# Layer 1's experts: outputs added as two float32r parts, the sum and the next gather placed between matrices, weight loads of one run per partition

## The chip, the cores and the metric

The kernel runs on one core of one Trainium2 chip. Its time is the device time of one execution in microseconds (us); the median of the runs shown counts. Engines: PE (TensorE; PEld is its weight load), DVE (VectorE), ACT (ScalarE), POOL (GpSimd), SP (SyncE, which issues the loads). "fp32" is float32; float32r is a second type that matmuls here are given; the kernel writes a float32 value as a sum hi + lo of two float32r values where it uses it.

## The reference

One sequence of 512 latent tokens and 256 context tokens of width 1024 goes through two layers (an mLSTM mixer and a retention mixer, each followed by experts) and then through a second block of another kind. What the change touches is the experts of layer 1, which act on the latent tokens alone:

```python
def expert_choice_ffn(h, router, w_gate, w_up, w_down):   # abridged: each of 16 experts picks its 64 best tokens
    aff = softmax(h @ router)                 # [512 tokens, 16 experts]
    gates, idx = top_k(aff.T, 64)             # an expert's 64 tokens and their gates
    xe = h[idx]                               # gather
    ye = (silu(xe @ w_gate) * (xe @ w_up)) @ w_down      # three matrices 1024 x 1024 of an expert
    return zeros.at[idx].add(gates[..., None] * ye)      # add to the tokens' rows
x = x + mod_l[5] * expert_choice_ffn(h_lat, ...)
```

Layer 0 does the same for 64 latent and 32 context tokens of an expert, and its mixer takes a shift and a scale, columns of `silu(c) @ ada_w[0]`.

## The kernel before

Layer 1's experts are `moe1`. X, the residual, lies in SBUF as four tiles of 128 tokens by 1024. Experts run one after the other; the first and the last stand alone for the gather, those between go in groups of two (1 and 2, 3 and 4, ...).

*Gather* (L1257). For a group a 0/1 matrix oh (L1249, DVE) picks the tokens, and per block of 128 features 4 matmuls bring the picked tokens, features on the partitions, into PSUM "tp" (three buffers), from where ACT (L1261) or DVE (L1259) writes them with gain and shift to xT (one buffer). 32 matmuls gather one group. *Facts* (L1279): small matmuls 64x17 that bring the gates and the numbers of the picked tokens, copied to mo_gi (L1281).

*Matrices* (`expert_gemm`, L866). A 1024x1024 matrix comes in four slots of 1 MiB, each one load on SP's queue (L833); a slot serves four matmuls of 64 tokens by 512 columns, and when they are done it is free for the next load. There are 18 slots. PSUM "pl" takes gate and up, "dl" down. Between up and down stands `expert_hidden`: silu on ACT (L1154), times up on DVE (L1155), four transposes (L1159) and a copy to hTl (L1160).

*Combine*. After down, y = dl * gate * mod5 goes to Y by two 64-partition DVE instructions (L1292); POOL copies the token numbers to ic (L1294). After each odd expert, so for a pair (0 and 1, 2 and 3, ...), a 0/1 matrix sh is made from ic (L1298, two DVE instructions), and for each of 8 pieces of X (4 token tiles by 2 halves of 512 columns) one float32 matmul sh x Y into PSUM "cb" (two buffers, L1302) and one DVE addition to X (L1304) follow:

```python
cb = ps.tile([128, 512], F32, name="cb", bufs=2)
nc.tensor.matmul(cb, sh[:, b, 128 * t:128 * t + 128], Y[b], start=True, stop=True)
nc.vector.tensor_add(xs, xs, cb)
```

What sets the order of the instructions is not the code alone: a scheduler of the tile framework orders each engine's instructions by what they depend on and by its own estimate of when things are ready, so that gathers come between the matmuls of a matrix in pieces. The order of each engine is fixed when the program is built. In the trace a float32 matmul 128x512 or 64x512 is two PE records (8 records are one slot of 4 matmuls), one of 128x128 also two, a float32r matmul one.

`ada_part` computes layer 0's shift and scale at the start, with two 512 KB loads per slot, of runs of 1 KB (L241).

Of the kernel before, what the change touches and what calls it, by code (L numbers as in the profile page):

```python
# [6 lines left out]
F32 = mybir.dt.float32  # L7
# [16 lines left out]
class Pool:  # L24
    """A tile pool that is closed by hand."""
# [11 lines left out]
class Ring:  # L37
    """Tiles of several pools in turn, as many of each as it has."""
# [9 lines left out]
class Net:  # L48
    NW = 4   # slots of the weight stream
    NB0, NB1 = (3, 3), (4, 2)   # slots beside them while the experts run, early and late, by layer  # L50
# [44 lines left out]
    def rstd(self, pool, ss, n, dim):  # L95
        """1 / sqrt(ss / dim + eps) for ss [128, n]."""
# [19 lines left out]
    def ada_open(self):  # L116
        """Pools of the modulation's products, which run beside other phases."""
# [20 lines left out]
    def fill(self, n=1):  # L138
        """Emits n steps, n may be a fraction, of the work that was put aside."""
# [10 lines left out]
    def ada_chunk(self, i, j, nr, p, tile):  # L150
        """Columns [1024 j, 1024 j + 1024) of silu(c) @ ada_w[i] + ada_b[i] for the first nr of both c:
        the products and their sum over row blocks on VectorE, a step a pair of them, the sum over partitions by
        tile(), of PSUM. The gates (j = 2 and 5) go to DRAM, else features are on the partitions."""
# [29 lines left out]
        else:  # L183
# [7 lines left out]
            # tp[:, 256 r + 128 b + 32 q + any]: block 2 q + b of the features, row r  # L191
# [12 lines left out]
    def ada_mix(self):  # L204
        """Of layer 1's mixer, the shift and scale; a step a row block."""
# [18 lines left out]
        # tp[:, 128 b + 64 c + 32 q + r]: chunk c, block 4 q + b of its columns, row r  # L224
# [34 lines left out]
    def load_weights(self, src):  # L259
        """src ([128, a, b] view of DRAM) in a slot."""  # L260
# [19 lines left out]
    def split_evac(self, pool, ps, hi, lo, A=None, B=None):  # L280
        """hi + lo = ps * A + B, from PSUM."""
# [11 lines left out]
    def mm3(nc, out, lh, rh, start, stop):  # L293
        """(lh0 + lh1)^T (rh0 + rh1) without the product of the low parts."""
# [61 lines left out]
    def normalise(self, pool, out, x, g=None):  # L356
        """out = x / rms(x) (* g), for a token tile [128, 1024]."""
# [129 lines left out]
    def mlstm_gates(self, G, gp):  # L487
        """Of both directions, what the chunks need of the gates, into self.gates: constants, and by direction the order of the
        chunks, the row terms (Fl - m, and exp(Fl - m + m before the chunk)) in three bfloat16 parts, and the
        columns ig - Fl, exp(suffix + ig - m at the end), exp(-m) and the state's decay."""  # L490
# [18 lines left out]
        def parts(x, name):  # L509
            """Three bfloat16 parts of x [8, 768] that add up to it, at partitions 0, 32 and 64."""  # L510
# [182 lines left out]
    def mlstm_finish(self, t, y, sigo, ng, pool):  # L693
        """Norm of each head of token tile t, times gain and sigmoid(o), in place."""
# [36 lines left out]
    def route_tile(self, x, r, dst, pp, ps, warm=None):  # L731
        """Softmax affinities of the token tile x [128, 1024] of kind r into dst [128, 16]; returns 1 / rms."""
# [8 lines left out]
        nc.scalar.activation(ss, self.epsc, AF.Sqrt)   # the function loaded ahead; ss is overwritten  # L741
# [23 lines left out]
    def rank_open(self, pp, kinds):  # L765
        """What the ranks of the first expert's tokens need: by kind of token, of which there are kinds[r] tiles."""
# [49 lines left out]
    def expert_stream(self, i, order):  # L816
        """The weights of layer i's experts, two row blocks of 128 a slot, by order: pairs of expert and matrix. open(slot, n,
        behind) starts loading into n further slots, once behind [1, 1] is there, not to hold up the load that brings it;
        get() is the next; done() frees the oldest one in use for a load."""
# [5 lines left out]
        def load(slot, behind=None):  # L825
# [7 lines left out]
            nc.sync.dma_start(t, I["moe_w_" + w][i, e, 128 * k:128 * k + 256, :].rearrange("(k p) n -> p k n", p=128))  # L833
# [1367 lines left out]
```

## Time and profile before

| | |
|---|---|
| runs, median (lowest to highest) | 2660.91 us, 3 runs (2656.61 to 2661.49) |
| profiled execution, first to last instruction | 2661.6 us |
| PE busy of it | 2543.3 us (96%) |
| DVE, ACT, POOL busy | 1069.2, 671.2, 564.7 us |
| mean granted clock of TensorE | 0.981 |
| bytes moved | 585.00 MB, 220 GB/s |

Layer 0's experts lie at 600 to 1100 us, layer 1's at 1517 to 2043 us, and the second block follows. A row of the windows gives for a stretch its length, each engine's busy time with its instructions in brackets, the granted clock as a share of full speed, the mean busy share of the 16 DMA engines and the bytes per time. A row of the waits gives the engine and line that waited, what released it, the total, the number of times and the longest. Idle time that the rows name is to the modelled end of the record before, so a gap read from start to start is longer.

### The profile page before, as it was taken

What the parts mean: (1) busy time and instruction counts of PE and PEld (TensorE: products, weight loads), DVE (VectorE), ACT (ScalarE), POOL (GpSimd) and SP (SyncE); (2) the same over time, 40 slices, a digit from 0 to 9 for tenths busy, and PEclk for the clock granted to TensorE, in tenths of its full rate; (3) what the DMA queues carried; (4) which work ended last, traced back from release to release, by engine and by line L of the source; (5) the groups of instructions that cost most, each with busy time, mean ns of one, the idle gap of its engine ahead of it and who ended that gap; (6) DMA issues with size and microseconds to landing.
All of it is one profiled execution on the core that took longest, in us unless ns stands there. A gap on an engine that the chain in (4) does not pass through costs nothing.

```text
span 2661.6 us, 36603 instructions
## 1 busy us (share of the span) xinstructions
PE 2543.3 (96%) x15126; PEld 1591.9 (60%) x15126; DVE 1069.2 (40%) x2072; ACT 671.2 (25%) x1303; POOL 564.7 (21%) x371
## 2 busy tenths in 40 slices
PE   7999998999999999999999999999998999999999
PEld 5777586833333333368777744444445766788887
DVE  5678687331111111053765432222224458533310
ACT  4332365421010111044224300000003436422211
POOL 2213224311111100024556100000001122122233
PEclk9999999989999999999999999999999999999999
DMA  7216604389999999432465599999992221133331
GB/s 249 80 50 210 236 14 168 129 331 330 387 387 390 390 388 387 132 133 70 175 221 187 192 383 406 392 388 385 391 376 81 97 91 41 48 98 101 119 103 56
DMA packets 201578, 585.00 MB, mean 220 GB/s; under 512 B 17655, under 2 KB 55583, under 8 KB 200388
## 3 DMA queue, kind: packets, MB, share of 16 engines
q1 hardware_dynamic: 194988, 570.07, 57.5%
q0 software_dynamic: 6416, 12.59, 2.2%
q8 instruction: 119, 1.95, 0.3%
q14 instruction: 47, 0.39, 0.0%
q10 hardware_dynamic: 8, 0.01, 0.0%
HBM read 567.90 MB, written 14.71 MB: 219 GB/s over the span
## 4 chain that ended last, share of the span: by engine, by line
PE 75%; issue 10%; DVE 9%; DMA 2%; ACT 2%; POOL 1%; SPq 0%; DVEq 0%; POOLq 0%; ACTq 0%
PE pl L866 14%; PE acc L297 11%; PE acc L296 11%; PE acc L295 11%; PE dl L866 4%; PE pc L871 3%; PE tp L1257 3%; PE ro_lg L866 3%; PE cb L1302 2%; DVE ada_v L164 2%; PE ro_lg L871 1%; DMA xl<-yl,mo_si 1%; PE o L670 1%; PE acc L113 1%; PE ro_lg L753 1%
## 5 line engine op out<-in xcount | busy, mean ns | idle before, releaser
L277 POOL TENSOR_TENSOR wlo<-w,whi 128x1024 fp32r<-128x1024 f32 x103 | 271.0, 2632 | 647.3 <-ACT whi L276 586.4
L866 PE MATMUL pl<-w,xT 128*64 128x512 f32 x1240 | 299.3, 600 | 0.0
L276 ACT ACTIVATE whi<-w 128x1024 fp32r<-128x1024 f32 x148 | 154.4, 1050 | 456.6 <-PE acc L297 194.2
L295 PE MATMUL acc<-whi,hhi 128*128 128x512 f32 (+2 forms) x672 | 266.4, 397 | 1.3 <-ACT pre L446 1.1
L296 PE MATMUL acc<-wlo,hhi 128*128 128x512 f32 (+2 forms) x672 | 262.2, 390 | 1.6 <-POOL wlo L277 1.6
L297 PE MATMUL acc<-whi,hlo 128*128 128x512 f32 (+2 forms) x672 | 261.1, 389 | 0.0
L297 PE MATMUL acc<-hhi,wlo 128*128 128x512 f32 (+2 forms) x528 | 200.2, 379 | 3.3 <-POOL wlo L277 3.2
L295 PE MATMUL acc<-hhi,whi 128*128 128x512 f32 (+2 forms) x528 | 199.5, 379 | 2.8 <-DVE hlo L290 1.4
L296 PE MATMUL acc<-hlo,whi 128*128 128x512 f32 (+2 forms) x528 | 200.2, 379 | 0.2 <-POOL hlo L407 0.2
L866 PEld LDWEIGHTS pl<-w,xT 128*64 128x64 f32 x1240 | 95.8, 136 | 139.4 <-issue 117.3
L277 DVE TENSOR_TENSOR wlo<-w,whi 128x1024 fp32r<-128x1024 f32 (+2 forms) x45 | 57.7, 1283 | 257.5 <-ACT whi L276 257.3
L866 PE MATMUL pl<-wb,xT 128*64 128x512 f32 x640 | 157.9, 599 | 0.0
L295 PEld LDWEIGHTS acc<-whi,hhi 128*128 128x128 f32 x672 | 127.9, 190 | 30.3 <-issue 6.1
L296 PEld LDWEIGHTS acc<-wlo,hhi 128*128 128x128 f32 x672 | 128.1, 191 | 27.3 <-POOL wlo L277 3.1
L297 PEld LDWEIGHTS acc<-whi,hlo 128*128 128x128 f32 x672 | 128.0, 191 | 26.0 <-issue 2.4
L164 DVE SCALAR_TENSOR_TENSOR ada_v<-w,csil,ada_v 128x1024 f32<-128x1024 f32 x84 | 130.1, 1583 | 8.9 <-DMA w<-in_ada_w_dram 7.6
L297 PEld LDWEIGHTS acc<-hhi,wlo 128*128 128x128 f32 (+1 forms) x528 | 98.9, 187 | 24.2 <-POOL wlo L277 3.4
L295 PEld LDWEIGHTS acc<-hhi,whi 128*128 128x128 f32 (+1 forms) x528 | 98.9, 188 | 22.0 <-DVE hlo L290 1.8
L1294 POOL COPY ic<-mo_gi 64x1 f32<-64x1 f32 x32 | 6.6, 207 | 492.9 <-DVE mo_gi L1281 458.1
L296 PEld LDWEIGHTS acc<-hlo,whi 128*128 128x128 f32 (+1 forms) x528 | 98.8, 187 | 20.3 <-issue 1.2
L1131 POOL DMA_INDIRECT xl<-yl,mo_si x16 | 25.1, 1569 | 362.9 <-DVE yl L1130 361.1
L1013 ACT ACTIVATE xT<-ro_tp,cols,ffnA 128x32 f32<-128x32 f32 x128 | 43.8, 377 | 223.8 <-DVE xT L1010 221.1
(594 smaller groups left out, 4225.9 us busy)
## 6 DMA issues: line engine op xcount, KB each, us to landing
w<-in_moe_w_gate_dram SPq DMA_DIRECT2D x91, 1024.0 KB
w<-in_moe_w_down_dram SPq DMA_DIRECT2D x84, 1024.0 KB
w<-in_moe_w_up_dram SPq DMA_DIRECT2D x68, 1024.0 KB
wb<-in_moe_w_up_dram SPq DMA_DIRECT2D x53, 1024.0 KB
w<-in_ada_w_dram SPq DMA_DIRECT2D x40, 1024.0 KB
wb<-in_moe_w_down_dram SPq DMA_DIRECT2D x38, 1024.0 KB
wb<-in_moe_w_gate_dram SPq DMA_DIRECT2D x30, 1024.0 KB
w<-in_ret_w_in_dram SPq DMA_DIRECT2D x16, 1024.0 KB
```

Source lines behind the costliest of these rows:

```text
L113: self.nc.tensor.matmul(out, self.identb if x.dtype == BF else self.ident, x, start=True, stop=True)
L164: nc.vector.scalar_tensor_tensor(acc[r], w[:, kk], x, acc[r], ALU.mult, ALU.add)
L276: nc.scalar.activation(hi, raw[:, k:k + n, :], AF.Copy)
L277: (nc.vector if fast and (k // n) % 2 == 0 else nc.gpsimd).tensor_sub(lo, raw[:, k:k + n, :], hi.bitcast(F32))
L295: nc.tensor.matmul(out, lh[0], rh[0], start=start, stop=False)
L296: nc.tensor.matmul(out, lh[0], rh[1], start=False, stop=False)
L297: nc.tensor.matmul(out, lh[1], rh[0], start=False, stop=stop)
L866: nc.tensor.matmul(outl[64 * b:64 * b + 64, :], lat(kk), w[:, kk - k0, 512 * c:512 * c + 512], start=kk == 0, stop=kk == KD - 1)
L871: nc.tensor.matmul(outc[32 * b:32 * b + 32, :], con(kk), w[:, kk - k0, 256 * b:256 * b + 256], start=kk == 0, stop=kk == KD - 1)
L1013: nc.scalar.activation(xT[:, kk, a:b], tp[:, k, a:b], AF.Identity, scale=A[:, kk, 1:2], bias=B[:, kk, 1:2])
L1257: nc.tensor.matmul(tp, y[:, t, 128 * k:128 * k + 128], oh[:, t, 0:m], start=t == 0, stop=t == 3)
L1302: nc.tensor.matmul(cb, sh[:, b, 128 * t:128 * t + 128], Y[b], start=True, stop=True)
```

## The change

1. *Layout.* The host stores the three expert arrays as [2, 16, 4, 128, 2, 1024], so that a load of 1 MiB reads one run of 8 KB for each partition instead of two of 4 KB, in both layers; and layer 0's shift and scale columns as an array `ada_mix0`, one load of 1 MiB per slot instead of two.
2. *Two parts.* y is written by one DVE instruction of 128 partitions (to the tile named hl, of which there is one); ACT copies it to Yhi (float32r, two instructions of 64 partitions), DVE subtracts to Ylo (two). ic comes from DVE instead of POOL. sh is float32r, made by two DVE comparisons with a broadcast operand, and shares its one buffer with the gather's oh. The combine has 16 float32r matmuls, hi and lo for each of the 8 pieces. Yhi and Ylo have one buffer each. The facts are 64x2 instead of 64x17.
3. *Places.* After up, either the next group's gather (first half before the transposes, second half and facts behind them) or the combine that is pending is written, instead of the gather inside the gate matrix and the combine right after down. At the end the pending ones are combined.

```diff
...
-            w = self.wslot().rearrange("p (k c n) -> p k c n", k=4, c=2)
-            for c in range(2):
-                nc.sync.dma_start(w[:, :, c, :], I["ada_w"][0, 128 * k:128 * k + 512, D * c + 256 * a:D * c + 256 * a + 256]
-                                  .rearrange("(k p) n -> p k n", p=128))
+            w = self.wslot()
+            nc.sync.dma_start(w, I["ada_mix0"][a, k // 4])
+            w = w.rearrange("p (k c n) -> p k c n", k=4, c=2)
...
             t = slot().rearrange("p (k n) -> p k n", k=2)
...
-            nc.sync.dma_start(t, I["moe_w_" + w][i, e, 128 * k:128 * k + 256, :].rearrange("(k p) n -> p k n", p=128))
+            nc.sync.dma_start(t, I["moe_w_" + w][i, e, k // 2])
...
     def moe1(self, yp, y):
...
-        iota = rp.tile([128, 516], F32, name="mo_iota")
+        iota = rp.tile([128, 129], F32, name="mo_iota")
+        num = rp.tile([128, 4], F32, name="mo_num")
+        off = rp.tile([128, 4], F32, name="mo_off")
...
-        gi = rp.tile([128, E, E + 1], F32, name="mo_gi")
+        gi = rp.tile([128, E, 2], F32, name="mo_gi")
...
+        nc.gpsimd.tensor_copy(at[:, :, E], num)
+        nc.vector.tensor_scalar(off, num, num[:, 0:1], None, ALU.subtract)
...
+        places = lambda dt: wk.tile([128, 2, 512], dt, name="sh", bufs=1)
...
+        xT = wk.tile([128, KD, 2, CL], F32, name="xT", bufs=1)
+        tp3 = lambda shape: ps.tile(shape, F32, name="tp", bufs=3)
+        def choose(e, m):
+            oh = places(F32)[:, 0, :].rearrange("p (t b c) -> p t b c", t=4, c=CL)
...
+            return oh
+        def gather(oh, e, m, ks):
...
+        def facts(oh, e, m):
...
+                        nc.tensor.matmul(tp[64 * b:64 * b + 64, a, :], oh[:, t, a, :],
+                                         at[:, t, e + a:E + 1:E - e - a], start=t == 0, stop=t == 3)
+            nc.vector.tensor_copy(gi[:, e:e + m], tp)
+        parts = []
+        def split(Y, dl, e, sw):
+            y = wk.tile([128, 512], F32, name="hl", bufs=1)
+            nc.vector.scalar_tensor_tensor(y, dl, gi[:, e, 0:1], m5[:, sw, :], ALU.mult, ALU.mult)
+            for b in range(2):
+                s = slice(64 * b, 64 * b + 64)
+                yh, yl = (x[s, b ^ sw, :] for x in Y)
+                nc.scalar.activation(yh, y[s, :], AF.Copy)
+                nc.vector.tensor_sub(yl, y[s, :], yh.bitcast(F32))
+        def combine():
+            (yh, yl), ic = parts.pop(0)
+            sh = places(F32R)
+            for b in range(2):
+                nc.vector.tensor_tensor(sh[:, b, :].rearrange("p (t n) -> p t n", t=4),
+                                        iota[:, None, 0:128].to_broadcast([128, 4, 128]),
+                                        ic[:, b, :, None].to_broadcast([128, 4, 128]), ALU.is_equal)
+            for t in range(4):
+                for b in range(2):
+                    cb = ps.tile([128, 512], F32, name="cb", bufs=2)
+                    s = sh[:, b, 128 * t:128 * t + 128]
+                    nc.tensor.matmul(cb, s, yh[:, b, :], start=True, stop=False)
+                    nc.tensor.matmul(cb, s, yl[:, b, :], start=False, stop=True)
+                    xs = X[:, t, 512 * b:512 * b + 512]
+                    nc.vector.tensor_add(xs, xs, cb)
+        oh = choose(0, 1)
+        gather(oh, 0, 1, range(4))
+        group = (0, 1)
+        Y = ic = None
+        for e in range(E):
+            e0, m = group
+            lat = lambda k: xT[:, k, e - e0, :]
             pl = [ps.tile([128, 512], F32, name="pl", bufs=2) for _ in range(2)]
             if e == 0:
-                self.route_rows(E, at, a, ps.tile([E, 512], F32, name="tp", bufs=3))
+                self.route_rows(E, at, a, tp3([E, 512]))
                 ranks()
-            self.expert_gemm(st, lambda k: xT[:, k, e - e0, :], None, pl[0], None,
-                             late=lambda k: gather((k + 2, k + 3)) if e == e0 and 2 <= k < KD - 2 else None)
+            self.expert_gemm(st, lat, None, pl[0], None,
+                             late=lambda k: gather(oh, 0, 1, (k + 2, k + 3)) if e == 0 and 2 <= k < KD - 2 else None)
+            hl = wk.tile([128, 512], F32, name="hl", bufs=1)
...
+                facts(oh, 0, 1)
+            self.expert_gemm(st, lat, None, pl[1], None)
+            nc.vector.tensor_tensor(hl, hl, pl[1], ALU.mult)
+            ahead = e + 1 < E and e + 1 == e0 + m
+            if ahead:
+                group = (e + 1, min(2, E - e - 1))
+                oh = choose(*group)
+                gather(oh, *group, range(4))
+            elif parts:
+                combine()
+            hTl = wk.tile([128, 4, 128], F32, name="hTl", bufs=1)
+            tp = tp3([128, 4, 128])
+            for b in range(4):
+                nc.tensor.transpose(tp[:, b, :], hl[:, 128 * b:128 * b + 128], self.ident)
+            nc.vector.tensor_copy(hTl, tp)
+            if ahead:
+                gather(oh, *group, range(4, KD))
+                facts(oh, *group)
             dl = ps.tile([128, 512], F32, name="dl")
             sw = e % 2
             self.expert_gemm(st, lambda k: hTl[:, k % 4, 64 * (k // 4):64 * (k // 4) + 64], None, dl, None, swap=sw)
             if sw == 0:
-                Y = [wk.tile([128, 512], F32, name=f"Y{b}", bufs=1) for b in range(2)]
-                ic = wk.tile([128, 2], F32, name="ic")
+                Y = [wk.tile([128, 2, 512], F32R, name=f"Y{x}", bufs=1) for x in ("hi", "lo")]
...
+            split(Y, dl, e, sw)
...
-                nc.vector.scalar_tensor_tensor(Y[b ^ sw][s, :], dl[s, :], gi[s, e, e:e + 1], m5[s, sw, :],
-                                               ALU.mult, ALU.mult)
-                nc.gpsimd.tensor_copy(ic[s, b ^ sw:1 + (b ^ sw)], gi[s, e, E:E + 1])
+                nc.vector.tensor_scalar(ic[s, b ^ sw, :], off[s], gi[s, e, 1:2], -1.0, ALU.subtract, ALU.mult)
             if sw:
...
+                parts.append((Y, ic))
+        while parts:
+            combine()
...
+    for w in ("gate", "up", "down"):
+        m = a["moe_w_" + w]
+        L, E = m.shape[:2]
+        out["moe_w_" + w] = np.ascontiguousarray(m.reshape(L, E, KD // 2, 2, 128, D).transpose(0, 1, 2, 4, 3, 5))
+    m = a["ada_w"][0, :, :2 * D].reshape(2, 4, 128, 2, 4, 256)
+    out["ada_mix0"] = np.ascontiguousarray(m.transpose(4, 0, 2, 1, 3, 5).reshape(4, 2, 128, 8 * 256))
...
```

The lines after are: gather L1249, its evacuation to xT L1251 (DVE) and L1253 (ACT), oh L1240, facts L1261 and L1263, y L1270, Yhi L1274, Ylo L1275, sh L1282, the matmuls L1289 (hi) and L1290 (lo), addition L1292, matrices L865, silu L1308, times up L1316, transposes L1328, hTl L1329, ic L1342.

PE's queue before, from the transposes of an odd expert (one of the later pairs): its down matrix, one matmul of the next expert's gate, and the combine.

```order
L1159 MATMUL tp<-cs,hl 128x128 x4
L866 MATMUL dl<-w_12839,hTl 64x512 x4
L866 MATMUL dl<-w_12845,hTl 64x512 x4
L866 MATMUL dl<-w_12851,hTl 64x512 x4
L866 MATMUL dl<-w_12857,hTl 64x512 x4
L866 MATMUL pl<-w_12863,xT 64x512
L1302 MATMUL cb<-Y_12906,sh 128x512
L1302 MATMUL cb<-Y_12907,sh 128x512
...
L866 MATMUL pl<-w_12863,xT 64x512 x3
```

All eight combine matmuls stand in one block, one matmul behind the end of down.

PE's queue after, from the transposes of the even expert that follows such a pair: gather and facts of the next group, the even expert's down, then the next gate, with the combine of the pair before among them.

```order
L1328 MATMUL tp<-cs,hl 128x128 x4
L1249 MATMUL tp<-sh,rt_y 128x128 x16
L1261 MATMUL tp<-mo_at,sh 64x2 x16
L865 MATMUL dl<-w_13322,hTl 64x512 x4
L865 MATMUL dl<-w_13328,hTl 64x512 x4
L865 MATMUL dl<-w_13336,hTl 64x512 x4
L1289 MATMUL cb<-Yhi,sh 128x512
L1290 MATMUL cb<-Ylo,sh 128x512
L865 MATMUL dl<-w_13342,hTl 64x512 x4
L1289 MATMUL cb<-Yhi,sh 128x512
L1290 MATMUL cb<-Ylo,sh 128x512
L1289 MATMUL cb<-Yhi,sh 128x512
```

The combine moved by nearly a whole expert and is cut into pieces by slots of matrix work; the gather stands in one piece of 16 behind the transposes.

PE's queue after, from the odd expert's transposes to the even expert's: the first gather blocks lie in the odd expert's down, a fourth in the even expert's up.

```order
L1328 MATMUL tp<-cs,hl 128x128 x4
L1249 MATMUL tp<-sh,rt_y 128x128 x4
L865 MATMUL dl<-w_13155,hTl 64x512 x4
L1249 MATMUL tp<-sh,rt_y 128x128 x3
L865 MATMUL dl<-w_13161,hTl 64x512 x4
L1249 MATMUL tp<-sh,rt_y 128x128 x5
L865 MATMUL dl<-wb,hTl 64x512 x8
L865 MATMUL pl<-w,xT 64x512 x16
L865 MATMUL pl<-wb,xT 64x512 x4
L1249 MATMUL tp<-sh,rt_y 128x128 x4
L865 MATMUL pl<-wb,xT 64x512 x12
L1328 MATMUL tp<-cs,hl 128x128 x4
```

Here the fourth block (x4 in the up matrix) comes once three PSUM buffers are taken by the first three.

DVE's queue after, around the combine, with the engines that each instruction waits for; before, the eight additions stood in one piece behind the two Y instructions.

```order
L1282 TENSOR_TENSOR sh<-mo_iota,ic 128x512 x2
L1342 TENSOR_SCALAR ic<-mo_off,mo_gi 64x4 [waits DVE_49]
...
L1292 TENSOR_TENSOR X<-X,cb 128x512 [waits PE_49]
L1270 SCALAR_TENSOR_TENSOR hl<-dl,mo_gi,mo_m_11569 128x512 [waits PE_49]
L1292 TENSOR_TENSOR X<-X,cb 128x512 [waits PE_49] x6
L1275 TENSOR_TENSOR Ylo<-hl,Yhi 64x512 [waits PE_49,Activation_49]
L1275 TENSOR_TENSOR Ylo<-hl,Yhi 64x512 [waits Activation_49]
L1292 TENSOR_TENSOR X<-X,cb 128x512
L1240 TENSOR_TENSOR sh<-mo_iota,mo_rk 128x128 x4
L1316 TENSOR_TENSOR hl<-hl,pl 128x512 [waits PE_49,Activation_49]
```

The even expert's y (written to hl) waits for the end of its down between the first and the second addition.

## Rows read from the trace of the kernel before

**Rows 1.** Windows: length; PE, PEld, DVE, ACT, POOL busy; clock; DMA share; GB/s

```profile
284.00:290.00 6.00, 4.63 (x27) 3.25 (x25) 6.00 (x6) 0.00 (x0) 0.00 (x0) 1.00 1.01 416
600.00:1100.00 500.00, 500.00 (x4180) 168.59 (x4178) 76.98 (x182) 56.79 (x154) 55.33 (x40) 1.00 0.98 366
1517.00:2043.00 526.00, 500.27 (x2568) 232.95 (x2568) 138.35 (x256) 37.89 (x70) 12.05 (x34) 1.00 0.93 361
1707.50:1772.50 65.00, 61.74 (x313) 28.35 (x313) 14.78 (x27) 3.02 (x6) 0.83 (x4) 1.00 0.99 388
1600.00:1700.00 100.00, 96.47 (x532) 46.30 (x530) 22.55 (x44) 5.46 (x11) 1.66 (x8) 1.00 1.03 408
```

**Rows 2.** Waits, 1517 to 2043: total us, times, longest

```profile
PEld cb L1302 <- DVE X L1304: 34.5, 48, 2.8
...
PE cb L1302 <- DVE Y L1292: 5.4, 6, 1.6
PE dl L866 <- DVE hTl L1160: 4.7, 6, 0.8
```

**Rows 3.** Waits of SP's queue, 1517 to 2030

```profile
SPq L833 <- PE pl L866: 263.0, 118, 10.7
```

**Rows 4.** Lines by shape, 1517 to 2043: count, busy, mean ns, idle before

```profile
L1304 DVE TENSOR_TENSOR X<-X,cb 128x512 f32<-128x512 f32 x64 | 43.7, 686 | 22.1 <-PE cb L1302 22.1
...
L1292 DVE SCALAR_TENSOR_TENSOR Y<-dl,mo_gi,mo_m 64x512 f32<-64x512 f32 x32 | 24.0, 750 | 88.2 <-PE dl L866 88.0
...
L1261 ACT ACTIVATE xT<-tp,cols,ffnA 128x128 f32<-128x128 f32 x28 | 12.8, 458 | 165.9 <-PE tp L1257 165.9
...
L1160 DVE COPY hTl<-tp 128x512 f32<-128x512 f32 x16 | 11.1, 692 | 12.0 <-PE tp L1159 12.0
...
L1298 DVE TENSOR_SCALAR sh<-mo_iota,ic 128x512 f32<-128x512 f32 x16 | 7.1, 481 | 1.4 <-POOL ic L1294 0.8
```

**Rows 5.** Timeline of PE, a later pair: start, length, records, idle before

```profile
1707.50 7.70 PE L1302 MATMUL cb<-Y,sh 128*128 128x512 f32 x16 [0.77 <-DVE Y L1292]
1715.13 2.37 PE L866 MATMUL pl<-w,xT 128*64 128x512 f32 x10
...
1744.35 1.94 PE L866 MATMUL pl<-w,xT 128*64 128x512 f32 x8
1746.22 1.83 PE L1257 MATMUL tp<-oh,rt_y 128*128 128x128 f32 x14
...
1754.22 3.80 PE L866 MATMUL pl<-wb,xT 128*64 128x512 f32 x16
1757.65 3.80 PE L866 MATMUL pl<-w,xT 128*64 128x512 f32 x16
1762.31 0.65 PE L1159 MATMUL tp<-cs,hl 128*128 128x128 f32 x4 [0.85 <-DVE hl L1155]
1763.75 3.65 PE L866 MATMUL dl<-w,hTl 128*64 128x512 f32 x16 [0.79 <-DVE hTl L1160]
...
1770.66 1.02 PE L866 MATMUL pl<-wb,xT 128*64 128x512 f32 x2
1772.45 1.12 PE L1302 MATMUL cb<-Y,sh 128*128 128x512 f32 x2 [0.77 <-DVE Y L1292]
```

**Rows 6.** Timeline of PE, 2399.9 to 2401.7: float32r products

```profile
2399.97 0.39 PE L295 MATMUL acc<-hhi,whi 128*128 128x512 f32 x1
...
2401.55 0.39 PE L296 MATMUL acc<-hlo,whi 128*128 128x512 f32 x1
```

**Rows 7.** Timeline of PE, the end of the experts

```profile
2022.11 7.09 PE L866 MATMUL dl<-w,hTl 128*64 128x512 f32 x32 [0.78 <-DVE hTl L1160]
2030.81 3.17 PE L1302 MATMUL cb<-Y,sh 128*128 128x512 f32 x6 [1.61 <-DVE Y L1292]
...
2049.61 0.28 PE L296 MATMUL acc<-wlo,hhi 128*128 128x256 f32 x1
2049.87 0.33 PE L1664 MATMUL tT_tp<-cs,s_sq 128*128 128x128 f32 x1
```

More of the change, by code (lines that the diff above doesn't have):

```diff
@@ L1148, in moe0 @@
         rp.close()
-    def expert_hidden(self, wk, ps, pl):
-        nc = self.nc
-        hl = wk.tile([128, 512], F32, name="hl", bufs=1)
-        nc.scalar.activation(hl, pl[0], AF.Silu)
-        nc.vector.tensor_tensor(hl, hl, pl[1], ALU.mult)
-        hTl = wk.tile([128, 4, 128], F32, name="hTl", bufs=1)
-        tp = ps.tile([128, 4, 128], F32, name="tp", bufs=3)
-        for b in range(4):
-            nc.tensor.transpose(tp[:, b, :], hl[:, 128 * b:128 * b + 128], self.ident)
-        nc.vector.tensor_copy(hTl, tp)
-        return hTl
     def moe1(self, yp, y):
@@ L1186, in moe1 @@
             nc.sync.dma_start(X[:, t, :], self.xl[128 * t:128 * t + 128, :])
-        nc.sync.dma_start(iota, I["iota"][:, 0:516])
+        nc.sync.dma_start(iota, I["iota"][:, 0:129])
+        nc.sync.dma_start(num, I["iota"][:, 512:516])
         self.rank_open(pp, (4,))
@@ L1210, in moe1 @@
         self.rank_sum(0, rk0)
-        nc.gpsimd.tensor_copy(at[:, :, E], iota[:, 512:516])
+        nc.gpsimd.tensor_copy(at[:, :, E], num)
+        nc.vector.tensor_scalar(off, num, num[:, 0:1], None, ALU.subtract)
         psum.close()
@@ L1222, in moe1 @@
         more()
-        rows = wk.tile([128, 2, 512], F32, name="sh", bufs=1)
+        places = lambda dt: wk.tile([128, 2, 512], dt, name="sh", bufs=1)
+        rows = wk.tile([128, 2, 512], F32, name="Yhi", bufs=1)
         a, rank = rows[0:E, 0, :], rows[0:E, 1, :]
@@ L1240, in moe1 @@
         A, B = self.ffnA[i], self.cols[i][:, 3]
-        Y = [None, None]
-        for e in range(E):
-            if e == 0 or e % 2:
-                e0, m = e, 1 if e in (0, E - 1) else 2
-                oh = wk.tile([128, 4, 2, CL], F32, name="oh", bufs=1)
-                for t in range(4):
-                    n, r = (1, rk[:, t, e:e + m]) if e else (0, rk0[:, t:t + 1])
-                    nc.vector.tensor_tensor(oh[:, t, 0:m], iota[:, None, n:n + CL].to_broadcast([128, m, CL]),
-                                            r[:, :, None].to_broadcast([128, m, CL]), ALU.is_equal)
-                xT = wk.tile([128, KD, 2, CL], F32, name="xT", bufs=1)
-                def gather(ks):
-                    for k in ks:
-                        tp = ps.tile([128, 4, CL], F32, name="tp", bufs=3)[:, 0:m]
-                        for t in range(4):
-                            nc.tensor.matmul(tp, y[:, t, 128 * k:128 * k + 128], oh[:, t, 0:m], start=t == 0, stop=t == 3)
-                        if k % 2 and e:
-                            nc.vector.tensor_scalar(xT[:, k, 0:m], tp, A[:, k, 0:1], B[:, k, 0:1], ALU.mult, ALU.add)
-                        else:
-                            nc.scalar.activation(xT[:, k, 0:m], tp, AF.Identity, scale=A[:, k, 0:1], bias=B[:, k, 0:1])
-                gather(range(4))
@@ new lines, in moe1 @@
+        xT = wk.tile([128, KD, 2, CL], F32, name="xT", bufs=1)
[3 more added lines that the diff above has]
+            for t in range(4):
+                n, r = (1, rk[:, t, e:e + m]) if e else (0, rk0[:, t:t + 1])
+                nc.vector.tensor_tensor(oh[:, t, 0:m], iota[:, None, n:n + CL].to_broadcast([128, m, CL]),
+                                        r[:, :, None].to_broadcast([128, m, CL]), ALU.is_equal)
+            return oh
@@ new lines, in gather @@
+        def gather(oh, e, m, ks):
+            for k in ks:
+                tp = tp3([128, 4, CL])[:, 0:m]
+                for t in range(4):
+                    nc.tensor.matmul(tp, y[:, t, 128 * k:128 * k + 128], oh[:, t, 0:m], start=t == 0, stop=t == 3)
+                if k % 2 and e:
+                    nc.vector.tensor_scalar(xT[:, k, 0:m], tp, A[:, k, 0:1], B[:, k, 0:1], ALU.mult, ALU.add)
+                else:
+                    nc.scalar.activation(xT[:, k, 0:m], tp, AF.Identity, scale=A[:, k, 0:1], bias=B[:, k, 0:1])
@@ new lines, in facts @@
+        def facts(oh, e, m):
+            tp = tp3([128, 4, 2])[:, 0:m]
+            for a in range(m):
+                for b in range(2):
+                    for t in range(4):
+                        nc.tensor.matmul(tp[64 * b:64 * b + 64, a, :], oh[:, t, a, :],
[10 more added lines that the diff above has]
+                nc.vector.tensor_sub(yl, y[s, :], yh.bitcast(F32))
@@ new lines, in combine @@
+        def combine():
[5 more added lines that the diff above has]
+                                        ic[:, b, :, None].to_broadcast([128, 4, 128]), ALU.is_equal)
+            for t in range(4):
+                for b in range(2):
+                    cb = ps.tile([128, 512], F32, name="cb", bufs=2)
[4 more added lines that the diff above has]
+                    nc.vector.tensor_add(xs, xs, cb)
@@ L1269, in moe1 @@
             if e == 0:
-                tr = ps.tile([128, 4, E], F32, name="tp", bufs=3)
+                tr = tp3([128, 4, E])
                 for t in range(4):
@@ L1273, in moe1 @@
                 nc.vector.tensor_copy(rk, tr)
-            if e == e0:
-                tp = ps.tile([128, 4, E + 1], F32, name="tp", bufs=3)[:, 0:m]
-                for a in range(m):
-                    for b in range(2):
-                        for t in range(4):
-                            nc.tensor.matmul(tp[64 * b:64 * b + 64, a, :], oh[:, t, a, :], at[:, t, :],
-                                             start=t == 0, stop=t == 3)
-                nc.vector.tensor_copy(gi[:, e:e + m], tp)
-            self.expert_gemm(st, lambda k: xT[:, k, e - e0, :], None, pl[1], None)
-            hTl = self.expert_hidden(wk, ps, pl)
+                facts(oh, 0, 1)
[16 more added lines that the diff above has]
+                facts(oh, *group)
             dl = ps.tile([128, 512], F32, name="dl")
@@ L1287, in moe1 @@
             if sw == 0:
-                Y = [wk.tile([128, 512], F32, name=f"Y{b}", bufs=1) for b in range(2)]
-                ic = wk.tile([128, 2], F32, name="ic")
+                Y = [wk.tile([128, 2, 512], F32R, name=f"Y{x}", bufs=1) for x in ("hi", "lo")]
+                ic = wk.tile([128, 2, 4], F32, name="ic")
+            split(Y, dl, e, sw)
             for b in range(2):
                 s = slice(64 * b, 64 * b + 64)
-                nc.vector.scalar_tensor_tensor(Y[b ^ sw][s, :], dl[s, :], gi[s, e, e:e + 1], m5[s, sw, :],
-                                               ALU.mult, ALU.mult)
-                nc.gpsimd.tensor_copy(ic[s, b ^ sw:1 + (b ^ sw)], gi[s, e, E:E + 1])
+                nc.vector.tensor_scalar(ic[s, b ^ sw, :], off[s], gi[s, e, 1:2], -1.0, ALU.subtract, ALU.mult)
             if sw:
-                sh = wk.tile([128, 2, 512], F32, name="sh", bufs=1)
-                for b in range(2):
-                    nc.vector.tensor_scalar(sh[:, b, :], iota[:, 0:512], ic[:, b:b + 1], None, ALU.is_equal)
-                for t in range(4):
-                    for b in range(2):
-                        cb = ps.tile([128, 512], F32, name="cb", bufs=2)
-                        nc.tensor.matmul(cb, sh[:, b, 128 * t:128 * t + 128], Y[b], start=True, stop=True)
-                        xs = X[:, t, 512 * b:512 * b + 512]
-                        nc.vector.tensor_add(xs, xs, cb)
+                parts.append((Y, ic))
+        while parts:
+            combine()
         ps.close()
```

1 line of the change is left out of this document (added).

## Prediction

> **What bounds the kernel now.** I read the windows first, to see stage by stage which engine is full. Layer 0's experts (600 to 1100) have PE busy 500.00 of 500 us: only fewer PE instructions could shorten them, and the change takes none there. Layer 1's experts (1517 to 2043) have PE busy 500 of 526 us at full granted clock, DMA share 0.93 [rows 1]. The DMA queue's waits come next: SP waits for PE to free a slot, 118 times for 263 us [rows 3], so weights are ahead of PE. With 18 slots of 1 MiB and 408 GB/s in the fullest stretch [rows 1] the lead can be 18 x 1.05 / 408 = 46 us. So PE's own queue sets the time: its matmuls and the gaps in which it waits for DVE.
>
> The timeline of one late pair of experts shows both [rows 5]. The pair lasts from 1707.50 to 1772.45, 64.95 us. In it the combine takes 7.63 us (1707.50 to 1715.13), though PE is paced by DVE there: eight additions of 0.686 [rows 4], cb having two buffers, and the weight loads of the combine wait 34.5 us for additions [rows 2]. A float32 matmul of 512 columns takes 0.429 us: 16 records in 3.43 us (1754.22 to 1757.65), 8 matmuls. Before the combine, two records of gate (0.43 from 1770.66) should end at 1771.09, and the combine begins at 1772.45: 1.36 us of waiting for Y. Transposes begin 1762.31 where the 16 records from 1757.65 end at 1761.08: 1.23 us of waiting for hl. From there to down (1763.75) are 1.44 us, of which four transposes at 0.126 (14 records, 7 matmuls, of the gather are 1.76 us, 1746.22 to the next slot at 1747.98, so 0.126 a record) explain 0.5: 0.95 waits for hTl. A slot of 8 records is 8 x 0.214 = 1.715, but followed by the gather 1.87 (1744.35 to 1746.22): a change from 64-row to 128-row work costs 0.155. These are the prices.
>
> **The change part by part**
>
> *Layout.* Loads of 8 KB a partition move faster: 416 GB/s in a stretch of such loads (the modulation's weights, share 1.01) against 408 with 4 KB (share 1.03), per unit of share 412 against 396, 4% [rows 1]. PE doesn't wait for weights, so I take nothing, in both layers. What hides it is the lead of slots; without that cover it is the third rival. The Trainium skill (DMA: Bandwidth & Descriptors, section Why small descriptors are slow) says that a packet pays some 3 cycles beside one for each 32 bytes. By that rule, an estimate, 8 KB would gain about 1% over two of 4 KB; the trace shows 4%. Neither changes the sum.
> Layer 0's shift and scale: SP issues half as many loads, in a stage that ends on norms; zero, at most 0.5 us less.
>
> *(a) Combine.* Seven of eight blocks lie inside the stream (the eighth is the tail). Before: 7 x 7.63 = 53.4. After, 16 float32r products each. Their pace here is 0.226 us (2399.97 to 2401.55, seven steps, both parts as operands [rows 6]): 16 x 0.226 = 3.6. In the order the block is cut in about four pieces by slots of matrix work: additions pass under these, but the first addition is followed on DVE by the even expert's y, which waits for the end of its down, so I allow two waits of an addition's length, 1.4, and four changes, 0.6: 5.6. Six such blocks and one at expert 3 that stands in one piece (paced by additions as before, 6.5) make 40.1: **-13.3**. Bounds: if float32r mixed with float32 costs the float32 pace of 0.429, the price is 7 x 16 x 0.203 = 23 more; if no addition is waited for, 8 less. I take 0.226, the only float32r rows.
>
> *(b) The wait for Y* stands before the combine at five late pairs (the early ones have a slot of gate in between) and goes, since the combine comes an expert later: 5 x 1.36 = **-6.8**. What is late next there is nothing of PE: ACT's copies and DVE's subtractions lie under the next expert's gather.
>
> *(c) The wait for hTl* counts six times [rows 2]; a gather piece now stands behind the transposes in five of these: 5 x 0.95 = **-4.8**.
>
> *(d) The wait for hl* (1.23, at thirteen of sixteen experts bare before) stays at eleven: at two the gather covers it (2.5), and two of the three shorter ones of about 0.6 go as well (1.2), -3.7; at expert 3 the silu, the product and two Ylo queue on DVE behind the last additions, 3.5 more: **-0.2**.
>
> *(e) A new wait.* xT has one buffer. A gather's fourth block stands in the even expert's up after 20 of its 32 matmuls of gate and up: it needs a tp buffer, which the first block's evacuation frees, which needs the even expert's last read of that part of xT, only a slot before. ACT's evacuation is 0.458 [rows 4], with the release that the 0.85 us before the transposes show [rows 5]: 4 x 0.85 = **+3.4**. Behind the waiting matmul stand only the rest of up. Zero to twice this.
>
> *(f) Fewer changes.* Gather, facts and transposes are entered from matrix work 58 times before and 35 after: 23 x 0.155 = **-3.6**. The facts are 17 or 2 columns; their pace is the instruction's, nothing.
>
> *New work on DVE and ACT.* Per pair two y of 128 partitions (0.75, half as many as before [rows 4]), four Ylo (0.69 to 0.75 by hTl and Y), two sh with a broadcast (0.48 by the old sh to 1.1), four ic of 0.15 to 0.3, four ACT copies (0.46 by xT to 0.75 by Y). DVE was busy 14.78 of 65 us [rows 1]; some 5 us more fit. They are hidden by matrix slots: sh has about 5 us of down between the facts, which free its buffer, and the first combine. If one chain is longer than that, it costs what it is longer; taken as zero, 0 to 1 us a pair.
>
> *(g) Tail.* The last combine waited 2022.11 + 7.09 to 2030.81 for Y, 1.6 [rows 7]; now y, copy and subtraction are in line (0.75 + 0.5 + 0.7 x 2 with releases, some 1.5 more), and the eight additions pace the rest as before: **+1.5**.
>
> Sum: -13.3 - 6.8 - 4.8 - 0.2 + 3.4 - 3.6 + 1.5 = -23.8. The profiled execution is 2661.6 us and gives 2637.8; the median of the runs is 0.7 lower, so **2637**.
>
> **Rivals**
>
> *1. The waits (a) and (e) vanish.* In (a) 6 x 1.4, in (e) 3.4: 12 us more, 2625. For it: DVE is free two thirds of the time. Against it: two cb buffers and an addition of 0.686 against 0.45 for a pair of products. Chance 0.14.
>
> *2. hi and lo cost what float32 did,* so that the change doesn't do what it says: 23 us more, 2660, no change. For it: no row shows a float32r product with float32 neighbours for a 0/1 operand. Against it: 0.226 in [rows 6] with both operands of this type. Chance 0.10.
>
> *3. The stream binds.* The new late pair is 64.95 - 2.0 - 1.4 - 0.95 + 0.85 - 0.5 = 61 us, for 65.0 x 388 = 25.2 MB, 413 GB/s. If the layout gave nothing, 408 would make it 61.8: 0.8 x 7 = 6 us, 2643. For it: share 0.99 in the pair already. Against it: a lead of up to 46 us and the faster 8 KB runs. Chance 0.06. By the 1% of the Trainium skill's page (412 GB/s, an estimate) it would be 1 to 2 us.
>
> *4. Slower: the one-buffer chain.* y, sh, Yhi and Ylo have one buffer each, and hl serves y and the next silu. If DVE's queue (additions, then Ylo that waits for PE to leave the old Ylo, then hl) stands in PE's line in every pair as at expert 3, a pair pays 6.5 + 3.5 = 10.0 instead of 5.6: 6 x 4.4 = 26 us, sum +2.6; with two further waits of 0.69 for Ylo in a pair, 7 x 1.4 = 9.7 more, +12: 2673. It decides from 24 / 7 = 3.4 us of new waiting a pair. For it: Ylo waits for PE behind six additions, and the seventh addition, which frees a cb, stands behind Ylo. Against it: 20 matmuls of matrix work (8.6 us) follow the last product before hl is needed. Chance 0.10. A change between float32 and float32r that costs more than shown would act alike: [rows 7] show 0.26 us from the last float32r product of 256 columns to a transpose, of which half a product's 0.226 is its own, so about 0.15 extra at most; some 60 such changes would need 0.4 us each to undo the gain.
>
> **How the numbers follow.** The forecast has 0.60; its own range, from (a) and (e) and the DVE chains at half or twice their size, is 2628 to 2648. The range for 8 in 10 reaches down to the first rival and up to the second: 2622 to 2660; outside remain the slower one (0.10), half of the second and a little below. 0.2% (5.3 us) is what can be told from no change. Faster by more: 0.60 + 0.14 + 0.06 and a little of the second, 0.81; within: 0.09; slower: 0.10.
>
> **What would show it.** In the changed profile: cb records at steps of 0.226 in pairs, and the time of PE's records of matrix work unchanged; late pairs of 61 us from one combine's first record to the next; the waits of cb for Y gone and of down for hTl down from six to one; a new wait of a tp matmul in up for ACT's xT of about 0.85; cb waits for DVE X near 1.4 us a pair. Layer 0's stage the same within 1 us. The forecast is wrong if cb steps are 0.43, if SP's waits for PE turn into PE waits for loads, or if the transposes' waits for hl grow beyond 1.5 us in each pair.

## The result and the profile after

The median is 2637.47 us (2628.87 to 2638.43, four runs) against 2658.76 (2655.21 to 2661.49): ratio 0.9913, 95% interval 0.9900 to 0.9927. The forecast was 2637. In the profiled executions the span goes from 2661.6 to 2636.3 us, by 25.3. It divides like this: the start of the first gather comes 0.9 us earlier (1517.07 to 1516.15); from there to the last expert's transposes 503.6 us become 476.7, 26.9 less; from these to the first float32r product of the second block 28.5 become 31.2, 2.7 more; the rest is 0.2 shorter.

The windows of the changed kernel, columns as in [rows 1]: layer 0's experts, and two late pairs from one combine's first record to the next.

```profile
600.00:1100.00 500.00, 500.00 (x4178) 168.62 (x4172) 75.76 (x180) 56.67 (x154) 53.67 (x39) 1.00 0.96 363
...
1729.84:1790.78 60.94, 58.22 (x313) 26.43 (x313) 16.77 (x33) 5.54 (x10) 0.00 (x0) 1.00 1.01 420
1790.78:1851.36 60.58, 58.22 (x314) 26.43 (x313) 16.77 (x33) 5.54 (x10) 0.00 (x0) 1.00 1.01 420
```

Layer 0's experts have PE full as before. A late pair takes 60.9 and 60.6 us instead of 64.95, at full clock, and the DMA queues deliver 420 GB/s where they gave 388.

The waits from the first gather to the end of the last down (total us, times, longest) answer to [rows 2].

```profile
PEld tp L1328 <- DVE hl L1316: 20.6, 12, 2.1
...
PEld cb L1289 <- DVE X L1292: 10.4, 16, 0.8
...
PE cb L1289 <- DVE X L1292: 3.9, 13, 0.3
PEld tp L1249 <- ACT xT L1253: 3.2, 4, 0.8
...
PE pl L865 <- ACT hl L1308: 2.7, 1, 2.7
...
PE dl L865 <- DVE hTl L1329: 0.8, 1, 0.8
```

Two PE waits of before are gone: none for Y (the tail's, 2.4 us for Yhi, lies behind this window), and that of down for hTl is one instead of six. The transposes still wait for hl. The combine's waits for additions are small (0.3 each on PE). One is new, once: gate for ACT's hl.

The timeline of PE in a late pair, answering to [rows 5]:

```profile
1790.78 0.50 PE L1289 MATMUL cb<-Yhi,sh 128*128 128x512 f32 x1
1791.12 0.39 PE L1290 MATMUL cb<-Ylo,sh 128*128 128x512 f32 x1
1791.44 1.94 PE L865 MATMUL dl<-wb,hTl 128*64 128x512 f32 x8
1793.30 0.50 PE L1289 MATMUL cb<-Yhi,sh 128*128 128x512 f32 x1
1793.64 0.40 PE L1290 MATMUL cb<-Ylo,sh 128*128 128x512 f32 x1
1793.88 0.39 PE L1289 MATMUL cb<-Yhi,sh 128*128 128x512 f32 x1
1794.10 0.40 PE L1290 MATMUL cb<-Ylo,sh 128*128 128x512 f32 x1
1794.43 1.94 PE L865 MATMUL pl<-w,xT 128*64 128x512 f32 x8
...
1797.81 0.50 PE L1289 MATMUL cb<-Yhi,sh 128*128 128x512 f32 x1 [0.32 <-DVE X L1292]
1798.24 1.94 PE L865 MATMUL pl<-w,xT 128*64 128x512 f32 x8
...
1804.11 1.94 PE L865 MATMUL pl<-w,xT 128*64 128x512 f32 x8
...
1851.36 0.50 PE L1289 MATMUL cb<-Yhi,sh 128*128 128x512 f32 x1
```

A piece of four products (1793.30 to 1794.43) takes 1.13 us, 0.56 for hi and lo with the changes to and from matrix work in it; the two inner steps, 0.24 and 0.23, make 0.46 without them. From 1790.78 to 1804.11 are 13.33 us with four slots of 1.715 between: the combine costs 6.47 us. The record at 1797.81 waits for an addition; so does a second one.

### The profile page after: what moved, and what is told of

It reads as the page before. It is cut to its first block, busy times and chain, and to the rows that moved or that the text cites. A ratio compares the mean times of both kernels' runs of the same rounds, so it can differ in the third digit from the quotient of the medians.

```text
span 2636.3 us, 36600 instructions
## 1 busy us (share of the span) xinstructions
PE 2516.1 (95%) x15122; PEld 1593.6 (60%) x15126; DVE 1089.3 (41%) x2121; ACT 690.5 (26%) x1335; POOL 557.1 (21%) x339
## 5 line engine op out<-in xcount | busy, mean ns | idle before, releaser
L865 PE MATMUL pl<-w,xT 128*64 128x512 f32 x1240 | 293.0, 601 | 2.7 <-ACT hl L1308 2.7
L865 PEld LDWEIGHTS pl<-w,xT 128*64 128x64 f32 x1240 | 86.2, 137 | 149.1 <-issue 133.1
L865 PE MATMUL pl<-wb,xT 128*64 128x512 f32 x640 | 152.8, 599 | 0.0
## 6 DMA issues: line engine op xcount, KB each, us to landing
wb<-in_moe_w_up_dram SPq DMA_DIRECT2D x53, 1024.0 KB, 13.3
```

The lines of the kernel that those rows point to most:

```text
L865: nc.tensor.matmul(outl[64 * b:64 * b + 64, :], lat(kk), w[:, kk - k0, 512 * c:512 * c + 512], start=kk == 0, stop=kk == KD - 1)
```

## The experiments

**The layouts alone, and all but the layouts.** The first puts the two loads and the host's re-layout into the kernel before, the second takes them out of the changed one:

```diff
-            nc.sync.dma_start(t, I["moe_w_" + w][i, e, 128 * k:128 * k + 256, :].rearrange("(k p) n -> p k n", p=128))
+            nc.sync.dma_start(t, I["moe_w_" + w][i, e, k // 2])
```

> The kernel before with the new layouts alone (expert weights as one 8 KB run per partition, layer 0's shift and scale as one load per slot); the experts of layer 1 as before. Theory (the weights are there before PE wants them): both expert stages keep their lengths within 1 us and late pairs stay at 64.9 us; the start of the program may gain some us, so 2653 to 2659 against 2658.8. Rival (the stream of weights is part of the bound): late pairs below 64.5 us and 2650 or less.

> The changed kernel with the old layouts of both arrays. Theory (the weights are there before PE wants them): late pairs stay at 60.6 us, 2637 to 2641, the difference from the start of the program alone. Rival (a pair of 60.6 us needs 415 GB/s, more than the 408 that runs of 4 KB gave): PE or SP waits for loads in the experts of layer 1, late pairs 61.8 us, 2643 to 2648.

The layouts alone: 2658.7 us against 2658.21, ratio 1.000 (0.9991 to 1.0009); from the first gather to the last transposes 503.6 us as before, late pairs 64.95. Without them: 2634.24, ratio 0.991 (0.9897 to 0.9924), a little below the range expected and not told apart from the changed kernel, with late pairs of 60.94 and 60.58 us as there. The window of 200 us in that run:

```profile
1700.00:1900.00 200.00, 191.70 (x1031) 87.09 (x1028) 54.27 (x107) 19.83 (x36) 0.00 (x0) 1.00 1.03 409
```

The queues are full at 409 GB/s, less than the 415 that such a pair needs (25.2 MB in 60.6 us), and PE does not wait: 3 us of shortfall in 200 us must come out of the lead of slots. The layout gave 420 instead of 409 GB/s and nothing of the time.

**Two parts in the old places.** The gather goes back into the gate matrix, and the combine directly behind the odd expert's down:

```diff
+            if e == 0 or e % 2:
+                oh = choose(e, m)
+                gather(oh, e, m, range(4))
...
                 parts.append((Y, ic))
+                combine()
```

> The changed kernel with two float32r parts, but gather and combine written where they stood before (gather in the group's first gate matrix, combine behind the odd expert's down). Theory (the places bring the gain; hi and lo together take 0.452 us, one float32 product took 0.429): the wait for Y at the late pairs grows from 1.36 to about 3 us, because copy and subtraction come behind y, and the combine is cut by two matmuls of gate between its pieces, so 2650 to 2658. Rival (the two parts bring the gain): 2640 to 2645.

2652.19 us, ratio 0.9971 (0.9959 to 0.9983): 6 us of the gain, as expected, though not for the reason given. PE, one late pair:

```profile
1707.45 0.72 PE L1289 MATMUL cb<-Yhi,sh 128*128 128x512 f32 x2 [1.31 <-ACT Yhi L1274]
...
1714.75 0.40 PE L1290 MATMUL cb<-Ylo,sh 128*128 128x512 f32 x1
...
1768.03 1.02 PE L865 MATMUL pl<-wb,xT 128*64 128x512 f32 x2
1770.37 0.73 PE L1289 MATMUL cb<-Yhi,sh 128*128 128x512 f32 x2 [1.31 <-ACT Yhi L1274]
```

From 1707.45 to 1715.08 are 7.63 us as before, but with 2.57 us of gate (six matmuls) inside: the products cost 2.6 us less. The combine waits from 1768.46 (two records from 1768.03) to 1770.37, 1.91 us instead of 1.36, for y, copy and subtraction; not 3. (0.43 of either number is the gate matmul itself, see (b) below.) The pair takes 62.92 us instead of 64.95.

**One part in the new places.**

```diff
-                    nc.tensor.matmul(cb, s, yh[:, b, :], start=True, stop=False)
-                    nc.tensor.matmul(cb, s, yl[:, b, :], start=False, stop=True)
+                    nc.tensor.matmul(cb, s, yh[:, b, :], start=True, stop=True)   # yh, s float32
```

> The changed kernel with its new places, but y as one float32 tile (by two DVE instructions of 64 partitions as before), sh float32 and one float32 product for each piece; no copy on ACT, no subtraction. Theory (places bring the gain, the split only adds work): combine products 8 x 0.429 = 3.4 us a pair instead of 16 x 0.228 = 3.65, no wait for the second part, no silu behind the subtraction at expert 3 (2.7 us), and the tail 2 to 3 us shorter: 2620 to 2630. Rival (float32r brings the gain): the combine falls back to 7.6 us a pair, 2650 or more.

2645.48 us, ratio 0.9951 (0.9937 to 0.9965): 15 to 25 us too little for the theory. The places bring 13 us, the parts 8 to 11 more on top (against 2637.47 and, without layouts, 2634.24). PE around two products, and the first records of two combines:

```profile
1731.27 1.94 PE L865 MATMUL pl<-w,xT 128*64 128x512 f32 x8
1733.14 1.98 PE L1285 MATMUL cb<-Yhi,sh 128*128 128x512 f32 x4
1735.05 1.94 PE L865 MATMUL pl<-w,xT 128*64 128x512 f32 x8
...
1790.58 1.12 PE L1285 MATMUL cb<-Yhi,sh 128*128 128x512 f32 x2
...
1853.49 1.13 PE L1285 MATMUL cb<-Yhi,sh 128*128 128x512 f32 x2
```

Four records, two float32 products, from 1733.14 to 1735.05: 1.91 us, of which 0.2 are the change of work. One product takes 0.856, not 0.429. No addition is waited for there, so this is PE's own time. The pair takes 62.91 us; its combine costs 8.8 (1790.58 to 1807.97 less five slots), against 6.47 with two parts.

**Half of each addition,** in the kernel before:

```diff
-                        xs = X[:, t, 512 * b:512 * b + 512]
-                        nc.vector.tensor_add(xs, xs, cb)
+                        xs = X[:, t, 512 * b:512 * b + 256]
+                        nc.vector.tensor_add(xs, xs, cb[:, 0:256])
```

> The kernel before with each addition to X over 256 of the 512 columns, which leaves out half of the experts' sum; the order of PE's instructions is the same. The prediction's view (the combine is paced by DVE's additions, products 0.429 us): with additions of about 0.4 us the block of eight falls from 7.63 to 4.5 us or less. Rival (a float32 product of 128 rows by 512 columns takes 0.856 us, as in the run with one part, so PE paces it: 8 x 0.856 = 6.85): the block stays at 6.9 to 7.63 us and late pairs stay within 0.7 us of 64.9.

2658.91 us in one run beside 2657.68 of the kernel before; one run doesn't tell a difference of some us. PE:

```profile
1706.43 1.02 PE L866 MATMUL pl<-w,xT 128*64 128x512 f32 x2
1708.22 7.13 PE L1302 MATMUL cb<-Y,sh 128*128 128x512 f32 x16 [0.77 <-DVE Y L1292]
1715.28 4.94 PE L866 MATMUL pl<-w,xT 128*64 128x512 f32 x22
```

The block of eight takes 7.06 us instead of 7.63, a late pair 64.38 instead of 64.95. So PE's products set its length before (8 x 0.856 = 6.85), and the additions of 0.686 hid under them but for 0.6 us.

**Cut by the slots of down.** The pair's combine goes into the next even expert's down, a token tile behind each slot:

```diff
+            piece = combiner() if parts else None
             self.expert_gemm(st, lambda k: hTl[...], None, dl, None, swap=sw,
+                             late=lambda k: piece(k // 2 - 1) if piece and k else None)
+            if piece:
+                piece(3)
```

> The changed kernel with the combine of a pair written into the next even expert's down matrix, one piece of four products (hi, lo, hi, lo) behind each of its four slots, so that it is over before that expert's y is split. Theory (two cb buffers hold two pieces of X, 1.72 us of matrix work between lets the additions of 0.686 pass): no wait for additions, a block 4.9 to 5.1 us instead of 6.5, and expert 3 loses its 2.9 us of waiting for silu: 5 x 1.5 + 3.6 = 11 us less than the changed kernel, 2623 to 2629. Rival (the wait moves to sh, which DVE makes between facts and the first piece, or to the order of DVE's queue): the first piece waits 1 us or more in each pair, 2632 to 2638.

2627.67 us, ratio 0.9889 (0.9872 to 0.9905). PE:

```profile
1780.05 0.50 PE L1290 MATMUL cb<-Yhi,sh 128*128 128x512 f32 x1
...
1781.17 1.94 PE L865 MATMUL dl<-w,hTl 128*64 128x512 f32 x8
...
1790.13 7.09 PE L865 MATMUL pl<-w,xT 128*64 128x512 f32 x32
...
1839.09 0.50 PE L1290 MATMUL cb<-Yhi,sh 128*128 128x512 f32 x1
```

From 1780.05 to 1790.13 with three slots between: 4.93 us of combine instead of 6.47; the pair takes 59.04. No PE record of the combine waits there, and expert 3 no longer waits for silu. A pair of 59.04 us needs 426 GB/s, and the queues gave 420 (1700 to 1900), so here the lead of slots shrinks even with the new layout; PE shows no wait for loads, and the old layout was not tried with this version. Both were run again together to compare them directly:

> The changed kernel once more, on the same chip as the next, to compare the two directly: 2634 to 2640.

> The kernel with the combine cut by the slots of the even expert's down, once more. Theory (five late blocks 1.5 us shorter, no wait for silu at expert 3): 8 to 12 us less than the changed kernel of the same call, 2624 to 2630. Rival (the earlier difference was chance): within 5 us of it.

2637.1 (0.9914, 0.9900 to 0.9927) and 2625.39 us (0.9868, 0.9854 to 0.9883): 11.7 us apart. This version beats both kernels.

**Three cb buffers,** tp two:

```diff
-                    cb = ps.tile([128, 512], F32, name="cb", bufs=2)
+                    cb = ps.tile([128, 512], F32, name="cb", bufs=3)
-        tp3 = lambda shape: ps.tile(shape, F32, name="tp", bufs=3)
+        tp3 = lambda shape: ps.tile(shape, F32, name="tp", bufs=2)
```

> The changed kernel with three cb buffers and two tp buffers instead of two and three (PSUM has eight banks). Theory (the waits for additions, 0.6 us twice a pair, come from two cb buffers): they go, a block takes 5.1 to 5.3 us, 6 to 8 us less, if the gather's blocks don't wait with two tp buffers. Rival (the gather needs three tp buffers): waits of tp for xT take it back, 2635 to 2645.

2633.47 us, ratio 0.9905 (0.9888 to 0.9921), told apart neither from the changed kernel nor from the 6 to 8 us less of the theory, so the traces must say. PE:

```profile
1790.83 0.50 PE L1289 MATMUL cb<-Yhi,sh 128*128 128x512 f32 x1
...
1800.89 3.65 PE L865 MATMUL pl<-w,xT 128*64 128x512 f32 x16
...
1850.42 0.50 PE L1289 MATMUL cb<-Yhi,sh 128*128 128x512 f32 x1
```

The waits for additions go, as the theory has it: 10.06 us less three slots, 4.9 of combine. The pair takes 59.59, 1.0 less; the other 0.5 is given back in the gather, whose pieces are cut otherwise with two tp buffers. Expert 3's wait stays.

## Why the prediction was right

Its mechanism is right in the main: the late pairs fall to 61 us, Y is waited for no more, and the float32r products run at their price. That the total lies within 1 us is luck: terms were off by up to 3.4 us in both directions and nearly cancel, four runs of the changed kernel spread over 10 us, and two readings were wrong. By its own steps, in the profiled executions:

| step | forecast | measured | from |
|---|---|---|---|
| (a) combine, seven blocks | -13.3 | -10.7 | 53.4 to 42.7 us |
| (b) wait for Y | -6.8 | -6.8 | gone at five pairs; 2.1 of it was no wait |
| (c) wait for hTl | -4.8 | -4.7 | six waits to one |
| (d) wait for hl | -0.2 | -2.2 | 5.1 less before transposes, 2.9 more at expert 3 |
| (e) new gather wait | +3.4 | 0 | below |
| (f) fewer changes | -3.6 | -2.5 | the rest of the 26.9, with the errors of the others |
| (g) tail | +1.5 | +2.7 | 28.5 to 31.2 |
| before and behind | 0 | -1.1 | 0.9 and 0.2 |

*The reading that failed* is the sentence that a float32 matmul of 512 columns takes 0.429 us and that PE "is paced by DVE there". 0.429 is the price of an expert's matmul, of 64 rows, which fills half of the output partitions; the next one fills the other half. The combine's product of 128 rows takes 0.856, as the runs with one part and with half additions show. So 7.63 was PE's time, and float32r cut it: 0.456 for hi and lo against 0.856. The Trainium skill (FP8 and Floating Point Precision, section TensorE Precision Notes) counts four passes for true FP32, and on the page TensorEngine Tiling (Array Packing), section Key Properties, it has different tiles of the array load and multiply in parallel. The rows agree: 0.856 is 3.8 times the 0.226 of [rows 6], and 64-row matmuls step at half of it. Set beside [rows 5], 16 records in 7.63 us, 0.477 each, should have raised the question. The error did not reach the sum, since (a) took the old block as a whole from the timeline and the new price from float32r rows. It made the second rival's price wrong (at 0.856 a product, 7 x 16 x 0.63 is 71 us, not 23; the run with one part, 8 to 11 us slower, is another case, with half as many products) and the reason: I thought the places brought all of (a). By the kernels the two parts in the old places give 6 us, the places with one part 13, both 21 to 24: the two nearly add up. In the late pairs shown parts alone and places alone save 2.0 us each and both together 4.4.

*(b)* has the right size, but 0.43 us of each 1.36 was PE's own work, not a wait; this is the second reading that failed. Two matmuls for different halves of the output partitions run side by side; one alone takes just as long. The last two records of an even expert's up, before (one matmul alone, its second record 0.43 behind its first) and after (two matmuls, one record of each):

```profile
1728.06 1.02 PE L866 MATMUL pl<-wb,xT 128*64 128x512 f32 x2
```

```profile
1812.32 0.60 PE L865 MATMUL pl<-wb,xT 128*64 128x512 f32 x2
```

Before, the combine stood behind one gate matmul ([rows 5], 1770.66), so this one ran alone, and from there to the end of up the halves were one matmul apart, so that another ran alone there. That cost 0.43 us in each of the five waits of (b) and 0.41 more before the transposes of five even experts: 4.2 us of the 26.9, half of it without a term in the prediction. The late pairs show it in the traces with the old places and not in those with the new ones, where the combine comes between whole slots; it was not tested by itself.

*(a)* has its two waits for additions, some 0.6 each with the restart, but the changes between matrix work and float32r cost 0.37 a piece (0.155 in, some 0.1 at the first product and 0.1 back), with four or five pieces (the Trainium skill, TensorEngine Tiling (Array Packing), section Key Properties, says that a change of tiling mode drains TensorE; the rows give the price here): 6.47 instead of 5.6 (the seven blocks: 5.7 at expert 3, then 6.1, four of 6.47 and 4.9). The regular cut of the last even expert's block, and of all blocks in the version cut by slots, shows 4.9.

*(d)* Of the 5.1 us less before the transposes 2.3 come from the gather that covers three of them (3.7 was forecast) and 2.1 from the halves in step again, as said; 1.1 is the facts, which left the halves 0.2 out of step before and now do so before a combine's first product, in (f); one wait is 0.35 longer. At expert 3 it came as forecast in kind: the silu waits for the one hl tile, from the last product to the next matmul of gate 2.9 us.

```profile
1622.21 0.50 PE L1289 MATMUL cb<-Yhi,sh 128*128 128x512 f32 x1
...
1627.67 0.39 PE L1290 MATMUL cb<-Ylo,sh 128*128 128x512 f32 x1
1630.78 1.97 PE L865 MATMUL pl<-w,xT 128*64 128x512 f32 x2 [2.72 <-ACT hl L1308]
```

*(e)* did not come. PE and ACT in an even expert's up:

```profile
1710.00 1.89 PE L865 MATMUL pl<-wb,xT 128*64 128x512 f32 x8
1711.08 0.46 ACT L1253 ACTIVATE xT<-tp,cols,ffnA 128x128 f32<-128x128 f32 x1 [0.26 <-PE pl L865]
1711.82 1.16 PE L1249 MATMUL tp<-sh,rt_y 128*128 128x128 f32 x8
1712.91 5.37 PE L865 MATMUL pl<-wb,xT 128*64 128x512 f32 x24
```

From 1710.00 the slot and the change take 1.82 us, as without a wait (1.87). The prediction let ACT start behind the whole slot; but the first part of xT is read by the first two of its four matmuls, and ACT's evacuation (1711.08 to 1711.54) ran beside the other two (0.86 us). The weight load of the gather did wait for it (four times, 0.8 each in the waits above).

*(g)* PE at the end of the experts, and two rows of DVE:

```profile
1992.88 0.66 PE L1328 MATMUL tp<-cs,hl 128*128 128x128 f32 x4 [0.86 <-DVE hl L1316]
1994.32 7.09 PE L865 MATMUL dl<-w,hTl 128*64 128x512 f32 x32 [0.78 <-DVE hTl L1329]
2003.79 0.73 PE L1289 MATMUL cb<-Yhi,sh 128*128 128x512 f32 x2 [2.38 <-ACT Yhi L1274]
...
2010.93 0.39 PE L1290 MATMUL cb<-Ylo,sh 128*128 128x512 f32 x1
2018.37 2.90 PE L113 MATMUL acc<-s_r,cs 128*128 128x128 f32 x12 [7.05 <-DVE s_r L1769]
...
2024.03 0.39 PE L294 MATMUL acc<-whi,hhi 128*128 128x272 f32 x1 [0.25 <-ACT hhi L288]
```

```profile
2011.96 2.84 DVE L1766 TENSOR_TENSOR X<-X,s_gf 128x1024 f32<-128x1024 f32 x1
...
2014.80 3.36 DVE L276 TENSOR_TENSOR wlo<-w,whi 128x1088 fp32r<-128x1088 f32 x1
```

The combine starts 2.4 us after down instead of 1.6, its last product starts 18.1 us after the transposes instead of 20.3, and then PE waits 7 us for s_r, which stands on DVE behind a subtraction of the second block's weights that took 3.36 us; another of the same shape took 1.29. Tails of the kernels with two parts took 29.2 to 31.5 us, of those with one part 26.7 to 28.5. That the split lengthens the tail is shown; that it does so by where DVE's queue meets POOL's work is read from the trace alone and was not tested.

The rivals: the first (no waits in (a) and (e)) came half true, (e) alone. The second did not come. The stream did not bind. The chain of one-buffer tiles cost 2.9 us at one place only.

## What to carry to other kernels

Price an operation by a row of the same shape: a matmul that fills half of the output partitions is no price for one that fills all. Before saying which engine paces a block, divide it by its instructions and compare with each engine's own duration. Where matmuls of two halves run side by side, put other work behind a pair of them: one left alone cost 0.43 us, here twice in a late pair. Where a block is hidden in another's slots, its pieces should be what the buffers hold (here two PSUM tiles): written that way by hand the same work took 1.5 us less a pair than in the scheduler's order.

## What the runs showed of the hardware

- A float32 product 128x128x512 took 0.856 us, the float32r one 0.228, so a split in two parts took 0.456.
- Two float32 matmuls of 64 rows for different halves of the output partitions ran side by side (two records in 0.60 us); one alone took as long as both (its two records 1.02).
- Full DMA queues gave 420 GB/s with runs of 8 KB and 409 with 4 KB (window of 200 us each), and a shortfall of 1.5% against PE's pace showed in no wait of PE.
- A DVE subtraction 128x1088 begun at 2014.80 took 3.36 us beside a subtraction 128x1024 on POOL (2013.68 to 2017.01), and 1.29 elsewhere.
